# Two layers of a diffusion backbone: the first two copies of a batch of DRAM sums issued later, four modulation tiles taken from the gate-up run into the output run, and the first weight sum of retention issued amid the token sums

## The chip, the core and the metric

The kernel runs on one core of a Trainium2 chip. The metric is the time of one execution on the device in microseconds (us), lower is better. The engines are named as in the profile: PE multiplies matrices, DVE works on vectors, ACT casts and evaluates functions, POOL (here mostly an issuer of transfers) and SP (an issuer only) have instruction queues of their own, and 16 DMA engines move what all of them issue.

## The reference

Two layers over 512 latent tokens and 256 context tokens of width 1024, all in float32. Layer 0 mixes tokens by windowed attention, layer 1 by retention in four heads. Each layer has a SwiGLU feed-forward with 2816 hidden columns, and each is modulated by rows computed from the condition vectors.

```python
for i in range(DEPTH):
    mx = jnp.split(c_act @ ada_w[i] + ada_b[i], 6, axis=-1)     # latent stream
    mc = jnp.split(cc_act @ ada_w[i] + ada_b[i], 6, axis=-1)    # context stream
    h_x = modulate(rms_norm(x, norm1_g[i]), mx[0], mx[1])
    h_c = modulate(rms_norm(y_ctx, norm1_g[i]), mc[0], mc[1])
    out_c, out_x = windowed_gqa_sink(...) if i == 0 else bidir_retention(...)
    x = x + mx[2] * out_x
    x = x + mx[5] * swiglu(modulate(rms_norm(x, norm2_g[i]), mx[3], mx[4]), ffn_w_in[i], ffn_w_out[i])
    # the same for y_ctx with mc, in layer 0 only
return x
```

## The kernel before

**Arithmetic.** A float32 product is made of three matmuls: each operand is split into a high part (a cast, on ACT, line 171 of the profile: `whi` of a weight, `aq` or `sA` of tokens) and a low part (the operand less its high part, on DVE, line 172: `wlo` and so on), and high x high, low x high and high x low are added up. Large products are done by a seven-product scheme instead of eight, so sums of weight blocks and of token blocks are needed beside the blocks. Weight sums are formed in three ways: by DRAM to DRAM transfers ahead of their use (`gu_sum`, `fo_sum`: a copy at line 827, then accumulating transfers at line 830), by an accumulating load (`add_chunk`, issued on POOL), or by an addition on DVE.

**Stages.** The start loads x and the context, squares x on ACT, and reads the first modulation tiles (up to some 70 us). Attention follows, then the feed-forward of layer 0. Its gate-up half for hidden tiles 2 to 21 is the "seven run" (`seven(pos, jobs)`, line 1164, about 412 to 711 us): 20 positions of seven products of twelve matmuls each. After every second position the pair's sums are formed on DVE (`pair_sums`, line 1059, called from `last_gate` of the position after) and four transfers on POOL store them in DRAM (`saved`, lines 1069 and 1071). Its output half is the "output run" (the loop over `FO`, about 711 to 874 us): seven products of eleven hidden pairs, two pairs to a step, so that steps m = 0 to 4 have 24 matmuls and step m = 5 has 12. Step i+2 is split on ACT and DVE while step i runs on PE. Layer 1 follows: the retention heads (from about 874 us) and its feed-forward.

**The order.** In the seven run and the output run all engines run in the order in which the code is written (`manual_schedule`). In retention a scheduler sets the order, and `after(a, [b])` keeps a behind b.

**Sums in DRAM.** `spread(steps, turns)` lays the eight transfers of a batch of `fo_sum` out over turns. Turns from 100 on are positions of the seven run: the transfers of turn 100 + pos are issued on POOL at the end of position pos, behind whatever POOL was given before. The second batch (five pairs, 1280 KB a transfer) begins with two copies from the weights, which wait for nothing.

**Modulation tiles.** Layer 1 needs 48 tiles of 1024 x 128 of its modulation matrix (`ada_q`). The first 32 alternate between tiles for both streams (two DVE instructions at line 284) and for one stream (one). All go through a single buffer, `adaw`: `ada_next` reduces the tile that is there on DVE, and then issues the load of the next one, which waits until DVE has read the old one. The load is issued on SP in the seven run and on POOL in the output run. Position pos takes one tile in job 0 (after the third product) and one in job 2 (at its end); the output run takes one after the splits of each of the steps m = 0, 2 and 4 of its products 0 to 4.

**Retention, head 0.** `token_sums` forms the sums of token blocks on DVE, four rounds k = 0 to 3, each with a split into `sA`. Its Y product needs these and `w2`, the parts of r11 + q12, where r11 and q12 are weight chunks and q12 has been loaded and added to (`add_chunk`). In the profile the addition is line 1723, the further sums are lines 1726 and 1727, and the matmuls are line 1582. `strips` evaluates the decay rows (`dx`, `dcx`) on ACT, line 108, from a table `rj` that SP loads.

Of the kernel before, what the change touches and what calls it, by code (L numbers as in the profile page):

```python
# [54 lines left out]
def dit_kernel(ctx, tc, xT, cT, crow, small, consts, masks, tabs0, tabs1, jtab, adaQ, adaN, adaT, wst, wgu, wfo, out):  # L55
    nc = tc.nc
    mult, add, sub = ALU.mult, ALU.add, ALU.subtract
# [9 lines left out]
    def T(pool, cols, tag, bufs, dt=F32):  # L67
        return pool.tile([P, cols], dt, tag=tag, bufs=bufs, name=tag)
# [757 lines left out]
    def sum_copy(dst, src, behind):  # L826
        after((nc.gpsimd if by_hand[0] else nc.sync).dma_start(flat(dst), flat(src), max_dma_last_dim=ROW), [behind] if behind else [])

    def sum_add(dst, src, behind):
        after(nc.gpsimd.dma_start(flat(dst), flat(src), accum_op=add, max_dma_last_dim=ROW), [behind] if behind else [])  # L830
# [7 lines left out]
    def fo_steps(b):  # L838
        rows = slice(sum(FO_BATCHES[:b]), sum(FO_BATCHES[:b + 1]))
        t = fo_sum[b]  # L840
        return [lambda a: sum_copy(t[3], wfo[0, rows], a), lambda a: sum_copy(t[2], wfo[2, rows], a),
                lambda a: sum_add(t[3], wfo[2, rows], a), lambda a: sum_add(t[2], wfo[3, rows], a),
                lambda a: sum_copy(t[0], t[3], a), lambda a: sum_add(t[0], wfo[3, rows], a),
                lambda a: sum_copy(t[1], t[0], a), lambda a: sum_add(t[1], wfo[1, rows], a)]
# [3 lines left out]
    def spread(steps, turns):  # L848
        for st, n in zip(steps, turns):
            sum_turns.setdefault(n, []).append(st)  # L850
# [3 lines left out]
    spread(gu_steps(2), (4, 4, 6, 7))  # L854
    spread(gu_steps(3), (8, 8, 9, 10))
    spread(fo_steps(0), (11, 11, 13, 14, 16, 17, 19, 21))
    spread(fo_steps(1), (103, 103, 105, 107, 109, 111, 113, 115))

    for st in sum_turns[-1]:
        st(keys_end)  # L860
# [164 lines left out]
    def token_sums():  # L1025

        h1, h2 = THIRDS
        for k in range(4):
            t1, t2 = tm[k], tm[k + 4]
            for j in (k, k + 4):  # L1030
                nc.scalar.activation(tm[j][:, h1], tm[j][:, h1], AF.Identity, bias=mods[0, 0][:, 3, j:j + 1])
            nc.vector.tensor_tensor(t2[:, h2], t1[:, h2], t2[:, h2], op=sub)
            nc.vector.tensor_tensor(t1[:, h2], t1[:, h1], t1[:, h2], op=sub)
            nc.vector.tensor_tensor(t1[:, h1], t2[:, h2], t1[:, h1], op=sub)
            nc.vector.tensor_tensor(park[:, k * 384:(k + 1) * 384], t2[:, h1], t1[:, h1], op=add)
            for n, t in ((1, t2[:, h2]), (3, t1[:, h2]), (2, t1[:, h1])):
                S[n, k] = parts(quarter())
                split(t, *S[n, k])
# [80 lines left out]
    def ada_next(behind=()):  # L1119

        args = ada_q.pop(0)
        ada_tile(*args, cr, behind, fp, ada_w.pop())
        ada_ahead()
# [201 lines left out]
    ada_q = [t for pair in zip(ada_both, ada_one) for t in pair] + ada_one[16:]  # L1325
# [20 lines left out]
    h_rest, h_first, hm, early, ctx_sum = [], [], [], [], []  # L1346
# [86 lines left out]
    def chunk(i, own=False):  # L1433
        raw = T(qw, 1024, "wx", 4) if own else T(rp, 1024, "wraw", 2)
        nc.sync.dma_start(raw, wst[i])
        return raw

    def add_chunk(raw, i):
        nc.gpsimd.dma_start(raw, wst[i], accum_op=add)

    def split_chunk(raw, behind=()):
        w = w_parts(hpool[0])
        last_split[0] = split(raw, *w, behind)
        return w
# [8 lines left out]
    with tc.manual_schedule(engines=Hand):  # L1453
        by_hand[0] = True
        for pos in range(2, FT):
            jobs = [nothing] * 3
            if pos == 2:
                jobs = [last_sum, gates_negated, nothing]
            elif pos == 3:
                jobs[0] = rows_begin  # L1460
            elif pos == 4:
                jobs[2] = rows_silu
                ada_ahead()
            else:
                cr = row_t[0]
                jobs[0] = jobs[2] = ada_next
            if pos == FT - 1:
                def begin():
                    fo_split_weights(0)
                    fo_split_tokens(0)  # L1470
                    fo_split_tokens(1)
                jobs[1] = begin
            end = seven(pos, jobs)
            for st in sum_turns.get(100 + pos, ()):
                st(None)
        fo_y = [bank("Y"), bank("Z"), bank("Z"), bank("Y")]
        o = fo_y
        for i, (prod, m) in enumerate(FO):
            if m == 0 and prod:
                o = fo_y if prod in (2, 4) else fo_z if prod == 5 else [bank("X"), bank("X"), pj(384), pj(384)] \  # L1480
                    if prod in (1, 3) else [bank("Y"), bank("Z"), bank("Z"), bank("Y")]
                if prod == 3:
                    fo_z = o
            if i == 0:
                fo_split_weights(1)
                last_gate(FT - 1)
            if i + 2 < len(FO) and i + 4 != len(FO) and i + 3 != len(FO):
                fo_split(i + 2)
            last = i == len(FO) - 2
            fo_step(i, o, prod in (0, 1, 3, 6), last)  # L1490
            if m == (PAIRS - 1) // 2:
                for args in (((0, 0),), ((0, 0),), ((4, 0, True),), ((4, 1),), ((4, 1, True), (0, 1)), ((4, 0),), ())[prod]:
                    fo_add(o, *args)
            if prod < 5:
                ada_next() if m % 2 == 0 and ada_q else None
            elif prod == 5:
                early_sums(m)
            else:
                late_sums(m)
            if last:  # L1500
                break
            if i == 2:
                Q.close()
                H = ExitStack()
                hpool[0] = H.enter_context(tc.tile_pool(name="hR", bufs=1, reuse_waits="tile", side="right"))
                h_rest += [(T(hpool[0], 512, "aq", 11, F32R), T(hpool[0], 512, "aq", 11, F32R)) for _ in range(4)]
                h_first += [T(hpool[0], 512, "aq", 11, F32R) for _ in range(3)]
                off_grid(hpool[0], 16)
                h_first.insert(0, T(hpool[0], 512, "aq0", 1, F32R))
                hm += [T(hpool[0], 512, "qk", 8) for _ in range(KT)]  # L1510
        fo_add(o, 0, 1)
        last_square = last_squares()
        b11.append(split_chunk(b11.pop()))
        by_hand[0] = False
# [10 lines left out]
    qp = R.enter_context(tc.tile_pool(name="qp", bufs=1, reuse_waits="tile"))  # L1525
# [3 lines left out]
    h_sum = [(T(hS, 512, "sA", 16, F32R), T(hS, 512, "sA", 16, F32R)) for _ in range(KT)]  # L1529
# [8 lines left out]
            return lambda k: first(4 * (n[1] == "2") + k, int(n[0]) - 1)  # L1538
        return of

    def token_sums(hm, part, sh2, sums, behind=(), ops=(add, sub)):

        q1, q2 = HALVES
        shift = mods[1, 0][:, part]
        plus, minus = ops
        nc.vector.tensor_tensor(sh2[:, 0:4], shift[:, 0:4], shift[:, 4:8], op=plus)
        for k in range(4):
            t1, t2 = hm[k], hm[k + 4]
            after(nc.vector.scalar_tensor_tensor(t2[:, q2], t1[:, q2], sh2[:, k:k + 1], t2[:, q2], add, plus), behind)
            nc.vector.tensor_tensor(t1[:, q2], t1[:, q1], t1[:, q2], op=sub)  # L1550
            nc.vector.scalar_tensor_tensor(t1[:, q1], t2[:, q2], shift[:, k:k + 1], t1[:, q1], sub, sub)
            mid = split(t1, *sums[2 * k + 1])
            nc.vector.scalar_tensor_tensor(t2[:, q1], t2[:, q1], shift[:, k + 4:k + 5], t1[:, q1], add, minus)
            other_sums.append((t2, *sums[2 * k]))
        return mid

    def other_parts():
# [112 lines left out]
    normed, other_rms = ends  # L1670
    latent_norm(1, range(KT))
    for hd in range(RH):
        bq = chunk_base + 16 * hd
# [17 lines left out]
            other_values()  # L1691
        r11, r21 = chunk(bq), chunk(bq + 1)
        k11, k21 = split_chunk(r11), split_chunk(r21)
        if hd == 0:
            sums = token_sums(hm, 0, T(qp, 16, "sh2", 1), h_sum, [normed], (sub, add))
            dx, dcx = strips(0, [sums], [other_rms])
        cos1, sin1 = rope_tables()
        Y, X, kc = W4("Y"), W4("X"), W4("X")
        kt, qt = [[T(qa, 512, "gate", 4) for _ in range(2)] for _ in range(2)]
# [18 lines left out]
            context_keys()  # L1718


        q12, q22 = chunk(bq + 2, True), chunk(bq + 3, True)
        add_chunk(q12, bq + 3)
        nc.vector.tensor_tensor(r11, q12, r11, op=add)
        w2 = split_chunk(r11, () if hd else [sums])
        other_parts()
        nc.vector.tensor_tensor(r21, r21, r11, op=add)
        nc.vector.tensor_tensor(r11, r11, q22, op=sub)
# [26 lines left out]
        g12, w2, w4 = [], [], []  # L1754
# [125 lines left out]
        if not last:  # L1880
            dx, dcx = strips(hd + 1)
# [79 lines left out]
        hm = [T(hM, 512, "hm", 8) for _ in range(KT)]  # L1961
# [49 lines left out]
    sh2 = T(fp, 48, "sh2", 1)  # L2011
# [272 lines left out]
```

## Time and profile before

| quantity | value |
|---|---|
| median of three runs | 1715.09 us (1711.99 to 1717.15) |
| time of the profiled execution | 1720.03 us |
| span in its profile | 1718.3 us |
| mean granted PE clock | 0.993 |
| PE busy | 1681.1 us, 98% of the span |
| DVE busy | 1340.4 us, 78% |
| ACT busy | 891.7 us, 52% |

Busy time counts work and not waiting. A row of the timeline gives start, duration, engine, line and operation, what is written <- what is read, and in brackets how long the engine stood idle before it and what released it. Rows of the waits sum such idle time: total, times, longest. Rows of the transfers give the issuing queue, the count, the size of one, and the time from issue to landing. In rows by stretch each engine has its busy time, then come the granted PE clock, the busy share of the DMA engines and what they moved in GB/s.

### The profile page before, as it was taken

The page shows a single profiled execution, that of the slowest core. Times are in us where ns is not written, and L with a number is a line of the kernel's source. Part 1 is how long each engine was busy: PE and PEld are TensorE (multiplying, and loading weights), DVE is VectorE, ACT ScalarE, POOL GpSimd, SP SyncE. Part 2 cuts the span into 40 slices and gives each one's busy share as a digit, 9 for nine tenths or more (in the row PEclk, how much of TensorE's full clock was granted, in tenths as well). Part 3 has the DMA queues.
Part 4 walks back from the last instruction along what each step waited for, and adds up shares of the span by engine and source line. Part 5 has one row for each costly group of instructions (what it writes and reads, how often), then busy time and mean ns, then how long its engine had stood idle before and what let it go on. Part 6 is the DMA issues. An engine that isn't in the chain of part 4 may idle for free.

```text
span 1718.3 us, 27884 instructions
## 1 busy us (share of the span) xinstructions
PE 1681.1 (98%) x10798; PEld 1524.0 (89%) x10798; DVE 1340.4 (78%) x2395; ACT 891.7 (52%) x1565; POOL 101.2 (6%) x219
## 2 busy tenths in 40 slices
PE   6999999999999999999999999999999999999999
PEld 3888887889999999999988888898898999999997
DVE  4798888788687988877789757757767898877774
ACT  4587888656444434444665534534535565444442
POOL 0001111000110100100000000000000000000000
PEclk8999999999999999999999999999999999999999
DMA  9849885634787786898653725624724324333322
GB/s 365 310 137 198 214 186 155 218 118 167 210 264 224 249 233 206 290 309 287 216 163 76 207 76 125 178 69 123 196 62 111 111 74 123 99 119 103 98 87 86
DMA packets 112036, 293.87 MB, mean 171 GB/s; under 512 B 9520, under 2 KB 20288, under 8 KB 111648
## 3 DMA queue, kind: packets, MB, share of 16 engines
q1 hardware_dynamic: 89536, 229.77, 41.0%
q0 software_dynamic: 22080, 61.81, 15.9%
q8 instruction: 84, 1.38, 0.3%
q10 hardware_dynamic: 288, 0.52, 0.1%
q14 instruction: 48, 0.39, 0.1%
HBM read 274.82 MB, written 61.28 MB: 196 GB/s over the span
## 4 chain that ended last, share of the span: by engine, by line
PE 81%; DMA 8%; DVE 7%; ACT 3%; issue 2%; DVEq 0%; SPq 0%; ACTq 0%
PE Y L971 13%; PE Z L971 7%; PE Z L1593 6%; PE pj L154 5%; PE pj L156 5%; PE pj L155 5%; PE Y L1582 3%; PE X L971 3%; PE Y L1266 2%; PE Z L1266 2%; PE S L727 2%; PE pT L753 2%; PE pO L775 2%; DVE wlo L172 2%; PE pj L1266 2%; PE X L1266 2%
## 5 line engine op out<-in xcount | busy, mean ns | idle before, releaser
L171 ACT CAST whi<-wraw 128x1024 fp32r<-128x1024 f32 (+1 forms) x284 | 294.1, 1040 | 302.6 <-PE Y L971 70.6
L172 DVE TENSOR_TENSOR wlo<-wraw,whi 128x1024 fp32r<-128x1024 f32 (+1 forms) x284 | 342.3, 1209 | 113.2 <-ACT whi L171 112.2
L971 PE MATMUL Y<-aq,whi 128*128 128x384 f32 x640 | 172.8, 335 | 0.0
L971 PEld LDWEIGHTS Y<-aq,whi 128*128 128x128 f32 x640 | 116.6, 188 | 0.0
L971 PE MATMUL Y<-aq,wlo 128*128 128x384 f32 x320 | 107.6, 336 | 4.5 <-DVE wlo L172 4.5
L284 DVE CUSTOM_DVE_ANT_0 y<-adaw,crow,small_sb 128x1024 bf16<-128x1024 f32 x64 | 82.1, 1282 | 31.7 <-DMA adaw<-in_adaT_dram 31.1
L1593 PE MATMUL Z<-whi,sA 128*128 128x512 f32 x256 | 80.7, 391 | 0.0
L108 ACT ACTIVATE pr<-pr,stat,qs 128x513 f32<-128x513 f32 (+2 forms) x96 | 74.1, 774 | 11.2 <-DVE stat L734 11.1
L154 PE MATMUL pj<-ax,whi 128*128 128x512 f32 x176 | 69.2, 393 | 0.9 <-DVE res L263 0.6
L156 PE MATMUL pj<-ax,whi 128*128 128x512 f32 x176 | 68.7, 390 | 0.0
L155 PE MATMUL pj<-ax,wlo 128*128 128x512 f32 x176 | 68.6, 390 | 0.0
L971 PEld LDWEIGHTS Y<-aq,wlo 128*128 128x128 f32 x320 | 60.2, 188 | 5.8 <-DVE wlo L172 5.8
L263 DVE SCALAR_TENSOR_TENSOR res<-pj,mod,res 128x512 f32<-128x512 f32 (+1 forms) x64 | 45.3, 713 | 16.9 <-PE pj L156 16.9
L971 PE MATMUL Y<-sA,whi 128*128 128x256 f32 x304 | 58.4, 277 | 0.0
L753 PE MATMUL pT<-const_sb,pr 128*128 128x128 f32 x352 | 56.3, 285 | 2.1 <-DVE pr L744 1.0
L728 DVE CUSTOM_DVE_ANT_0 pr<-S,mask,qs 128x256 f32<-128x256 f32 (+1 forms) x96 | 53.4, 568 | 5.3 <-PE S L727 4.4
L1593 PEld LDWEIGHTS Z<-whi,sA 128*128 128x128 f32 x256 | 48.0, 188 | 10.4
L971 PE MATMUL Y<-hx,whi 128*128 128x256 f32 x304 | 56.5, 278 | 0.0
L1266 PE MATMUL Y<-aq,whi 128*128 128x384 f32 x176 | 52.9, 337 | 0.0
L1266 PE MATMUL Z<-aq,whi 128*128 128x384 f32 x176 | 51.4, 334 | 0.0
L1593 PE MATMUL Z<-wlo,sA 128*128 128x512 f32 x128 | 50.5, 394 | 0.5 <-DVE wlo L172 0.5
L753 PEld LDWEIGHTS pT<-const_sb,pr 128*128 128x128 f32 x352 | 41.2, 145 | 11.1 <-issue 4.3
(602 smaller groups left out, 5086.3 us busy)
## 6 DMA issues: line engine op xcount, KB each, us to landing
wraw<-in_wst_dram SPq DMA_DIRECT2D x157, 512.0 KB, 3.7
adaw<-in_adaT_dram SPq DMA_DIRECT2D x39, 512.0 KB, 3.8
op<-saved SPq DMA_DIRECT2D x35, 384.0 KB, 5.4
saved<-op POOLq DMA_DIRECT2D x33, 384.0 KB, 3.6
wraw<-in_wgu_dram SPq DMA_DIRECT2D x24, 512.0 KB, 4.5
gu_sum<-in_wgu_dram SPq DMA_DIRECT2D x8, 1280.0 KB, 13.0
gu_sum<-in_wgu_dram POOLq DMA_DIRECT2D x8, 1280.0 KB, 12.9
wraw<-fo_sum SPq DMA_DIRECT2D x20, 512.0 KB, 4.9
```

Source lines behind the costliest of these rows:

```text
L108: ins = nc.scalar.activation(*args, **kw)
L154: nc.tensor.matmul(o, whi, xhi, start=first, stop=False)
L155: nc.tensor.matmul(o, wlo, xhi, start=False, stop=False)
L156: return nc.tensor.matmul(o, whi, xlo, start=False, stop=last)
L171: after(nc.scalar.copy(hi, t), behind)
L172: return nc.vector.tensor_tensor(lo, t, hi, op=sub)
L284: res.append(nc.vector.tensor_tensor_reduce(junk, w, cr[:, s * 1024:(s + 1) * 1024], 1.0, sm_t[:, C_ADAB + l * 48 + j:C_ADAB + l * 48 + j ...
L728: nc.vector.tensor_tensor_reduce(pt[:, c0:c0 + w], bank, mask[:, m0:m0 + w], 1.0, top, add, ALU.min, lo)
L753: nc.tensor.transpose(tp[:, a * P:(a + 1) * P], self.pr[(0, 2, 1, 3)[a]][:, ki * P:(ki + 1) * P], ident)
L971: nc.tensor.matmul(o, p, r, start=first and k + i == 0, stop=k == 3 and i == 2, skip_group_check=not first)
L1266: nc.tensor.matmul(o[d], p[:, ws], r, start=first and k + e == 0, stop=k == PAIRS - 1 and e == 2, skip_group_check=True)
L1593: ins = nc.tensor.matmul(os[t], p, r, start=first and k + i == 0, stop=k == 3 and i == 2, skip_group_check=by_k or not first)
```

## The change

Three edits, independent of each other.

1. The second batch of `fo_sum` is one turn later in each of its eight transfers.
2. Positions 7, 9, 13 and 17 of the seven run no longer take a modulation tile in job 0. The output run takes one more, behind step m = 3, in products 0 to 3.
3. In head 0 the weight sum (loads of q12 and q22, addition to r11, split) is called out of `token_sums` after its round k = 1; before, it stood behind the first three products and its cast behind all of `token_sums`. The strips' later rows wait for `normed` instead of `other_rms`.

```diff
-    spread(fo_steps(1), (103, 103, 105, 107, 109, 111, 113, 115))
+    spread(fo_steps(1), (104, 104, 106, 108, 110, 112, 114, 116))
...
-                jobs[0] = jobs[2] = ada_next
+                jobs[2] = ada_next
+                if pos not in (7, 9, 13, 17):
+                    jobs[0] = ada_next
...
-                ada_next() if m % 2 == 0 and ada_q else None
+                ada_next() if ada_q and (m % 2 == 0 or m == 3 and prod < 4) else None
...
-    def token_sums(hm, part, sh2, sums, behind=(), ops=(add, sub)):
+    def token_sums(hm, part, sh2, sums, behind=(), ops=(add, sub), amid=None):
...
+            if amid and k == 1:
+                amid()
         return mid
...
+        qx, w2 = [], []
+
+        def weight_sum():
+            qx.extend((chunk(bq + 2, True), chunk(bq + 3, True)))
+            add_chunk(qx[0], bq + 3)
+            nc.vector.tensor_tensor(r11, qx[0], r11, op=add)
+            w2.extend(split_chunk(r11))
+
         if hd == 0:
-            sums = token_sums(hm, 0, T(qp, 16, "sh2", 1), h_sum, [normed], (sub, add))
-            dx, dcx = strips(0, [sums], [other_rms])
+            sums = token_sums(hm, 0, T(qp, 16, "sh2", 1), h_sum, [normed], (sub, add), weight_sum)
+            dx, dcx = strips(0, [sums], [normed])
...
-        q12, q22 = chunk(bq + 2, True), chunk(bq + 3, True)
-        add_chunk(q12, bq + 3)
-        nc.vector.tensor_tensor(r11, q12, r11, op=add)
-        w2 = split_chunk(r11, () if hd else [sums])
+        if hd:
+            weight_sum()
+        q12, q22 = qx
```

**POOL's queue.** The difference on POOL, first at the program's start and then in the seven run; `off` are small constants, `saved` the stores of a pair, `fo_sum_1179` the second batch.

```order
 L237 MEMSET off_541 128x48
 L237 MEMSET off_544 128x16
-L827 DMA fo_sum_1179<-in_wfo_dram 640x512 x2
 L237 MEMSET off_978 128x16
 L711 COPY pr<-qs 128x1 x10
...
 L1069 DMA saved_4632<-op 128x2x384 x4
 L1071 DMA saved_4632<-op 128x384
-L830 DMA fo_sum_1179<-in_wfo_dram 640x512
+L827 DMA fo_sum_1179<-in_wfo_dram 640x512 x2
 L1069 DMA saved_4633<-op 128x2x384 x3
 L1071 DMA saved_4633<-op 128x384
```

Before, the two copies stand at the very start of the program: they wait for nothing, and no instruction that is ordered by hand stands ahead of them on POOL. Now they stand behind the second pair's stores, where the first accumulating transfer stood, and each later transfer stands one pair further on.

**DVE's queue in the output run.** Product 0 of the output run before, from its step m = 2 on: `wlo` and `aq` are the low parts of a step's weights and tokens, the two rows at line 284 one modulation tile, line 1285 the additions of the product to the residual.

```order
1183 L284 ISA y_8130,mod_76<-adaw,crow,small_sb 128x1024
1184 L284 ISA mod_76 128x1
1185 L172 TENSOR_TENSOR wlo<-wraw,whi 128x512
1186 L172 TENSOR_TENSOR aq<-op,aq 128x384
1187 L172 TENSOR_TENSOR wlo<-wraw,whi 128x1024
1188 L172 TENSOR_TENSOR aq<-op,aq 128x768
1189 L284 ISA y_8232,mod_76<-adaw,crow,small_sb 128x1024
1190 L284 ISA mod_76 128x1
1191 L172 TENSOR_TENSOR wlo<-wraw,whi 128x1024
1192 L172 TENSOR_TENSOR aq<-op,aq 128x768
```

The same place now:

```order
1175 L284 ISA y_8114,mod_76<-adaw,crow,small_sb 128x1024
1176 L284 ISA mod_76 128x1
1177 L172 TENSOR_TENSOR wlo<-wraw,whi 128x512
1178 L172 TENSOR_TENSOR aq<-op,aq 128x384
1179 L284 ISA y_8180,mod_76<-adaw,crow,small_sb 128x1024
1180 L284 ISA mod_76 128x1
1181 L172 TENSOR_TENSOR wlo<-wraw,whi 128x1024
1182 L172 TENSOR_TENSOR aq<-op,aq 128x768
1183 L284 ISA y_8220,mod_76<-adaw,crow,small_sb 128x1024
1184 L284 ISA mod_76 128x1
1185 L172 TENSOR_TENSOR wlo<-wraw,whi 128x1024
1186 L172 TENSOR_TENSOR aq<-op,aq 128x768
```

A third tile stands between the split of the half step (128x512) and the split of the next product's first step. The tile of step 0 of product 0, ahead of these rows, is now one for both streams where it was one for one stream.

**DVE's queue in head 0.** The token sums before (lines 1549 to 1553, splits into `sA` at line 172) and the weight sum behind them:

```order
1384 L172 TENSOR_TENSOR sA<-qk,sA 128x512
1385 L1553 SCALAR_TENSOR_TENSOR qk<-qk,mod_76 128x256
1386 L172 TENSOR_TENSOR sA<-qk,sA 128x512
1387 L1621 TENSOR_TENSOR hn<-hn,rj 128x256
1388 L1723 TENSOR_TENSOR wraw<-wx,wraw 128x1024
1389 L1622 TENSOR_TENSOR dx<-hn 128x128
1390 L172 TENSOR_TENSOR sA<-qk,sA 128x512
1391 L1726 TENSOR_TENSOR wraw<-wraw 128x1024
1392 L172 TENSOR_TENSOR wlo<-wraw,whi 128x1024
```

The place in the token sums where the same addition (now line 1703) and its split stand now:

```order
1376 L1555 SCALAR_TENSOR_TENSOR qk<-qk,mod_76 128x256 x2
1377 L172 TENSOR_TENSOR sA<-qk,sA 128x512
1378 L1703 TENSOR_TENSOR wraw<-wx,wraw 128x1024
1379 L172 TENSOR_TENSOR sA<-qk,sA 128x512
1380 L1551 SCALAR_TENSOR_TENSOR qk<-qk,sh_9921 128x256 x2
1381 L1552 TENSOR_TENSOR qk<-qk 128x256
1382 L172 TENSOR_TENSOR wlo<-wraw,whi 128x1024
1383 L1553 SCALAR_TENSOR_TENSOR qk<-qk,mod_76 128x256
```

The addition and the low part of its result (line 172, `wlo`) stand amid rounds 2 and 3 of the token sums, ahead of the strips' products (line 1621 before).

## The prediction

> **What bounds the kernel now.** I read the page's engine rows and chain first, then the waits of PE stage by stage, then, where PE waits, what ended that wait.
>
> ```profile
> PE 1681.1 (98%) x10798; PEld 1524.0 (89%) x10798; DVE 1340.4 (78%) x2395; ACT 891.7 (52%) x1565; POOL 101.2 (6%) x219
> PE 81%; DMA 8%; DVE 7%; ACT 3%; issue 2%; DVEq 0%; SPq 0%; ACTq 0%
> ```
>
> PE is busy 98% of the span, 37 us idle in all. The change touches no matmul, so it can gain or lose only where PE stands still or would stand still. Three places matter. The first is the start: the transfers of the first 70 us, two windows, and what PE waited for up to 120 us.
>
> ```profile
> DMA packets 8947, 26.20 MB, mean 374 GB/s; under 512 B 942, under 2 KB 1326, under 8 KB 8940
> q0 software_dynamic: 672, 2.62, 10.4%
> fo_sum<-in_wfo_dram POOLq DMA_DIRECT2D x2, 1280.0 KB, 13.9
> 15.00:20.00 5.00, 0.00 (x0) 0.00 (x0) 0.69 (x1) 1.02 (x2) 0.00 (x0) 0.55 1.01 383
> 30.00:50.00 20.00, 19.23 (x269) 15.73 (x269) 15.04 (x38) 9.89 (x21) 0.00 (x0) 1.00 1.02 395
> PE pT L227 <- DVE y L220: 9.7, 1, 9.7
> ```
>
> All DMA engines are busy, and PE waits 9.7 us for the sum of squares; ACT's last square shows why:
>
> ```profile
> 19.61 0.63 ACT L219 ACTIVATE hs<-res 128x512 f32<-128x512 f32 x1 [2.75 <-DMA res<-in_xT_dram]
> 21.02 2.08 PE L227 MATMUL pT<-y,ones_sb 128*128 128x512 f32 x2 [9.66 <-DVE y L220]
> 23.02 3.27 PE L356 MATMUL pT<-adan,ccol 128*32 128x128 f32 x64
> ```
>
> It waits for x itself. From 23 us on PE is nearly dense (19.23 of 20 us), so its start sets when it gets through.
>
> The second place is the output run. PE never waits in its middle, but DVE does, for modulation tiles; the window of one product, DVE's waits from 700 to 850 us, and the tile loads from 711 to 826 us:
>
> ```profile
> 734.00:757.00 23.00, 23.00 (x134) 23.00 (x134) 18.93 (x25) 10.10 (x13) 1.85 (x4) 1.00 0.91 308
> DVE y L284 <- DMA adaw<-in_adaT_dram: 9.5, 6, 3.0
> adaw<-in_adaT_dram POOLq DMA_DIRECT2D x14, 512.0 KB, 4.5
> ```
>
> The third is head 0, in PE's waits from 840 to 1010 us and three windows behind the longest, with the clock down to half:
>
> ```profile
> PE Y L1582 <- DVE wlo L172: 1.6, 1, 1.6
> PE Y L1582 <- ACT gate L1736: 0.8, 1, 0.8
> PE Y L1582 <- ACT whi L171: 0.6, 1, 0.6
> 912.00:914.00 2.00, 1.73 (x12) 1.73 (x13) 2.00 (x4) 0.06 (x2) 0.00 (x0) 0.81 0.00 0
> 914.00:916.00 2.00, 2.00 (x11) 2.00 (x11) 2.00 (x3) 1.04 (x1) 0.00 (x0) 0.50 0.00 0
> 916.00:918.00 2.00, 2.00 (x17) 2.00 (x17) 0.96 (x3) 1.22 (x2) 0.00 (x0) 0.84 0.39 59
> ```
>
> **Part 1, the copies leave the start.** They are all of POOL's 2.62 MB in the first 70 us and land 13.9 us after issue, while x is still being loaded. At 0.374 to 0.42 MB per us (the mean rate, and the best of the early windows) the bytes are 6.2 to 7.0 us of the engines' time; their share, 10.4% of 70 us, is 7.3. I take 6.5 off the time at which x, and every load behind it, lands: −6.5 us, from −5 (ACT's squares have work of their own between the waits) to −8.5.
>
> The low end of that range has this behind it: the granted clock is 0.55 from 15 to 20 us, where PE idles, and the first matmuls after it run slowly. A wait of 3 us in place of 9.7 may keep the clock up; L227 and L356 are 5.3 us together, so at most some 2 us come on top. The Trainium skill, TensorE: Matmul & The Clock Gate, Part 1, has the clock fall to half after an idle window of about 3.4 us; the trace agrees, with 0.55 behind 9.66 us of idling, and by that rule a wait of 3 us could go either way.
>
> The copies now run at about 449 us, where one accumulating transfer ran:
>
> ```profile
> 448.70 1.20 POOL L830 DMA_DIRECT2D fo_sum<-in_wfo_dram  x1
> L284 DVE CUSTOM_DVE_ANT_0 y<-adaw,crow,small_sb x64: 1277/1284/1286, 461.8 to 814.6; 128x1024 bf16<-128x1024 f32 x64
> 489.02 1.28 DVE L284 CUSTOM_DVE_ANT_0 y<-adaw,crow,small_sb 128x1024 bf16<-128x1024 f32 x1 [4.02 <-DMA adaw<-in_adaT_dram]
> PE Y L971 <- DVE wlo L172: 4.5, 4, 1.8
> ```
>
> Two copies move twice one transfer's bytes. The first tiles are read from 462 us, so a backlog until then costs at most a delay of 0.5 us; I take +0.5, from 0 to 1. The further transfers each move one pair on. Where they meet a pair's stores, a tile lands late, DVE waits (4.02 us at 489), the split behind it is late and PE waits: 4.5 us in four places in the whole run (the last row, 400 to 720 us). Position 16 gets such a meeting for the first time; by the others it is +1.
>
> **Part 2 in the seven run.** The dropped job-0 tiles come right behind the waiting tile of the position before, so they take none of those four waits away. They change which tiles are single: in positions 8, 14, 15 and 16 the first is now single and the second double. The second's load starts 1.28 us earlier and its reduction takes 1.28 longer, which cancels. Dropping four loads lightens the DMA engines a little: −1. The seven run's sum with position 16: 0, from −2.5 to +3.
>
> **Part 2 in the output run.** A tile's cycle, from rows of DVE and POOL:
>
> ```profile
> 718.34 1.28 DVE L284 CUSTOM_DVE_ANT_0 y<-adaw,crow,small_sb 128x1024 bf16<-128x1024 f32 x1
> 719.93 0.56 POOL L275 DMA_DIRECT2D adaw<-in_adaT_dram  x1 [1.93 <-DVE mod L284]
> 726.63 1.28 DVE L284 CUSTOM_DVE_ANT_0 y<-adaw,crow,small_sb 128x1024 bf16<-128x1024 f32 x1 [2.99 <-DMA adaw<-in_adaT_dram]
> 728.76 0.54 POOL L275 DMA_DIRECT2D adaw<-in_adaT_dram  x1 [8.28 <-DVE wlo L172]
> 734.47 1.28 DVE L284 CUSTOM_DVE_ANT_0 y<-adaw,crow,small_sb 128x1024 bf16<-128x1024 f32 x1 [2.99 <-DMA adaw<-in_adaT_dram]
> 735.67 1.22 DVE L172 TENSOR_TENSOR wlo<-wraw,whi 128x1024 fp32r<-128x1024 f32 x1
> 736.81 0.95 DVE L172 TENSOR_TENSOR aq<-op,aq 128x768 fp32r<-128x768 f32 x1
> 743.37 0.53 POOL L275 DMA_DIRECT2D adaw<-in_adaT_dram  x1 [6.78 <-DVE mod L284]
> 747.50 1.28 DVE L284 CUSTOM_DVE_ANT_0 y<-adaw,crow,small_sb 128x1024 bf16<-128x1024 f32 x1 [0.41 <-DMA adaw<-in_adaT_dram]
> ```
>
> With one buffer, the next load is issued 1.6 us after a tile's start (718.34 to 719.93), and the next tile can start 0.1 us after its landing. At the median landing of 4.5 us a cycle is 6.2 us. A product on PE is 132 matmuls of 23.00/134 = 0.172 us, about 22.8 us (4.15 a step, half that for the half step). Three cycles, 18.6 us, fit; four, 24.8, do not. The quoted waits of DVE show the scatter from issue to next tile: 719.93 to 726.63 is 6.7 us, 728.76 to 734.47 5.7, 743.37 to 747.50 4.1.
>
> The output run starts here:
>
> ```profile
> 711.20 0.33 PE L1266 MATMUL Y<-aq,whi 128*128 128x384 f32 x1
> ```
>
> The shortage reaches PE, since DVE takes its queue in order: the split of the next product's step 0 stands behind the new tile, and that of its step 1 behind the fourth. Worked once, for product 0 and landings of 4.5: tile m2 starts at 719.93 + 4.5 + 0.1 = 724.5, its successor's load is issued 2.1 later (as at 726.63 to 728.76), so the new tile starts at 731.3 and the split behind it ends at 731.3 + 1.2 + 1.15 + 0.9 = 734.6, where PE wants it at 711.2 + 22.8 = 734.0. The fourth tile starts 6.2 later, at 737.5; the split of step 1 ends at 740.7, where PE, 0.6 late by then, wants it at 738.8. Some 2 us more of waiting, and the next product begins as late.
>
> I replayed the five products so, step by step (DVE in order; 1.14 us for the low part of weights by the starts of the rows at 735.67 and 736.81, 0.87 for that of tokens, whose 0.95 overlaps the next; half for the half step; PE starting a step when both are there). With the landings of the trace the replay gives tiles at 726.6, 734.5, 747.5 and 755.1, the rows' own times, and no wait of PE, as in the profile. With four tiles PE's waits come to:
>
> ```
> landing, us      3.8   4.0   4.25  4.5   4.75  5.0
> PE waits, us     3.5   5.9   8.9  11.9  15.4  18.8
> ```
>
> With the trace's scatter of landings in place of one value it is 14 to 23, 18 in the middle, since a late tile costs and an early one gives little back. I take +12: the run is stretched by about a tenth, so the engines, at 0.91 here, are a little freer for each load. Clock dips behind such waits fall into the next wait and add nothing. The double tile in product 0 adds 1.28 us of DVE: +1. Together +13, from +4 to +20.
>
> **Part 3, head 0.** Rows of DVE and ACT before:
>
> ```profile
> 907.92 1.22 DVE L1723 TENSOR_TENSOR wraw<-wx,wraw 128x1024 f32<-128x1024 f32 x1
> 910.99 1.23 DVE L172 TENSOR_TENSOR wlo<-wraw,whi 128x1024 fp32r<-128x1024 f32 x1
> 915.07 1.22 DVE L172 TENSOR_TENSOR wlo<-wraw,whi 128x1024 fp32r<-128x1024 f32 x1
> 886.52 0.71 ACT L108 ACTIVATE dx<-rj,dcol 128x384 f32<-128x384 f32 x1 [2.31 <-DMA rj<-in_jtab_dram]
> ```
>
> The addition at 907.92, its cast and its low part are what PE waited for twice (0.6 and 1.6). They now come during X's product, and these waits go. The next weights' low part, at 915.07 + 1.22 = 916.3, moves up by about 2.5 us (1.22 + 1.23), as the addition and the low part ahead of it are done; so the copy of Y that held PE for 0.8 comes earlier too. The dip of the clock behind the waits (0.81, 0.50 and 0.84 in three windows of 2 us: 2 x (0.19 + 0.50 + 0.16) = 1.7 us) goes with them. ACT's 2.31 us of waiting for the table of the decay rows, with the casts behind it, also goes, since those rows now come later. The waits and the dip are 0.6 + 1.6 + 0.8 + 1.7 = 4.7; of this I let 0.9 come back, since DVE has the same work to do in the same stretch: −3.8, from −4.7 to −1.5.
>
> **The sum.** −6.5 + 0.5 + 0 + 13 − 3.8 = +3.2 us. The profiled execution, 1720.0, would become 1723.2; it is 4.9 above the median of the runs, and I set the same difference on the median: 1715.1 + 3.2, about 1718. What a measurement of this kernel can tell from no change is about 0.3%, 5.1 us.
>
> **The rivals.** The sum without the landings' term is 1 − 9.8 = −8.8 us, so the mean landing decides: 3.7 us or less gives faster by over 5.1, 4.65 or more slower by over 5.1.
>
> *Slower, by landings as they scatter.* One mechanism: in the output run, tile loads share the engines with step loads, as the 5.7 to 6.7 us above, and each late tile holds the splits behind it. +18 in place of +12 gives +9, 1724; it decides from a mean landing of 4.65 us. For: two of the three quoted gaps from issue to tile are far above the median. Against: a stretched run asks less of the engines per us.
>
> *Faster, by short landings.* With four loads spread over a longer product, landings of 3.8 to 4.0 give 3.5 to 5.9, and a clock kept up at the start another −2: −5 to −7, about 1709. For: one gap quoted above is 4.1 us, and loads of the same tile on SP land so, in the whole program:
>
> ```profile
> adaw<-in_adaT_dram SPq DMA_DIRECT2D x39, 512.0 KB, 3.8
> ```
>
> Against: 0.91 of the engines' time is taken in the output run.
>
> *The copies hold nothing up.* If x's loads kept their pace whatever POOL moves, part 1 would be worth 0 and the whole +9.7, 1725. Against it: full engines, and 13.9 us for 1.28 MB. The Trainium skill, DMA: Bandwidth & Descriptors, Queues, rings and completion order, says that an engine takes turns between its queues packet by packet; the trace agrees, with both queues moving side by side in those 14 us, and by that rule the copies take their share from x.
>
> **How the numbers follow.** The forecast, within 0.3%, takes landings of 3.8 to 4.6 and part 1 as costed: 0.37. Slower by over 0.3% is 0.35: 0.29 for scattered landings, 0.06 for copies that held nothing up. Faster is 0.28, by short landings and by sizes at the good ends of parts 1 and 3. The range goes from 1706, the faster rival with part 1 at −8.5, to 1727, the slower one with position 16 at +3.
>
> **What would show it.** Right: PE's first sum of squares (L227) at about 14.5 us; tiles in the output run 6 us apart and DVE waiting for them 30 us or more in all; PE waiting for `wlo` in steps 0 and 1 of products 1 to 4, about 3 us a product; Y's product in head 0 without the waits of 0.6 and 1.6. Wrong: PE dense through the output run, or L227 still near 21 us.

## The result, and the profile after

The changed kernel takes 1721.24 us (median of 6 runs, 1716.83 to 1723.45) against 1713.47 us of the kernel before in the same runs (6 runs, 1710.18 to 1717.15): 7.8 us more, a ratio of 1.004 with a 95% interval of 1.0021 to 1.0059. The time lies within the range given, 3 us above the forecast. It is a small loss, at the edge of what the 0.3% of the prediction can tell from no change.

Its profiled execution took 1723.45 us, the longest of the six. The page's first row, then the rows of PE's matmuls in the seven run and the output run (count, shortest/median/longest in ns, first and last start in us):

```profile
PE 1684.6 (98%) x10798; PEld 1523.2 (88%) x10798; DVE 1341.1 (78%) x2395; ACT 891.7 (52%) x1565; POOL 104.5 (6%) x223
L971 PE MATMUL Y<-aq,whi x640: 334/334/525, 402.0 to 705.2; 128*128 128x384 f32 x160
L1266 PE MATMUL Y<-aq,whi x176: 334/334/526, 705.4 to 882.6; 128*128 128x384 f32 x176
```

The busy shares say almost nothing: PE is busy 98% of the span before and after. The first and last starts of a stage say much, and I cut every profile at the same four places: the first matmul of the seven run, the first and the last of the output run, and the first of the last feed-forward (L154). Stages in us, with the kernels of the experiments, which are told below:

| kernel | start | seven run | output run | retention | rest |
|---|---|---|---|---|---|
| before | 412.6 | 298.6 | 163.1 | 534.2 | 309.8 |
| before, a second profile | 409.8 | 294.6 | 163.0 | 533.7 | 309.1 |
| changed | 402.0 | 303.4 | 177.2 | 530.2 | 308.6 |
| changed, a second profile | 401.4 | 300.9 | 176.9 | 530.5 | 308.6 |
| first edit alone (e1) | 402.5 | 299.0 | 163.1 | 533.9 | 310.6 |
| second edit alone (e2) | 408.8 | 299.6 | 176.3 | 533.9 | 308.6 |
| third edit alone (e3) | 409.4 | 296.7 | 163.0 | 531.0 | 309.6 |
| first and third (e4) | 402.6 | 296.8 | 163.0 | 530.2 | 310.4 |
| changed, four tiles not loaded (e5) | 401.6 | 303.6 | 163.1 | 530.0 | 309.9 |
| changed, four loads not waited for (e6) | 401.2 | 299.8 | 163.1 | 530.7 | 308.9 |
| before, copies behind x (e7) | 410.7 | 293.3 | 163.1 | 534.5 | 310.1 |
| first and third, sums held (e8) | 402.1 | 299.1 | 163.1 | 529.8 | 308.6 |
| changed, kinds of tiles put back (e9) | 401.7 | 298.8 | 178.5 | 531.0 | 308.6 |
| first and third, tile behind the splits (e10) | 401.1 | 301.0 | 165.3 | 530.3 | 310.7 |

Start, output run and retention repeat to a microsecond or so from profile to profile where the code is the same (the start with the copies in it to 4 us). The seven run scatters by 4 us with the same code, so one profile of it says little.

**The start.** The transfers of the first 70 us, the window from 10 to 15 us, and PE:

```profile
DMA packets 8649, 24.93 MB, mean 356 GB/s; under 512 B 960, under 2 KB 1344, under 8 KB 8640
10.00:15.00 5.00, 5.00 (x64) 2.79 (x66) 2.08 (x3) 3.36 (x6) 0.00 (x0) 1.00 1.03 419
12.53 1.04 PE L227 MATMUL pT<-y,ones_sb 128*128 128x512 f32 x2
13.49 1.97 PE L356 MATMUL pT<-adan,ccol 128*32 128x128 f32 x64
```

PE comes to the sum of squares at 12.5 instead of 21.0 us, without a wait, and the clock is 1.00 there: L227 and L356 take 3.0 us instead of 5.3.

**The seven run.** PE's wait, two of the six places that make it up, and the windows behind these two:

```profile
PE Y L971 <- DVE wlo L172: 8.6, 6, 2.8
603.77 0.44 PE L971 MATMUL Y<-aq,wlo 128*128 128x384 f32 x1 [2.75 <-DVE wlo L172]
636.79 0.45 PE L971 MATMUL Y<-aq,wlo 128*128 128x384 f32 x1 [2.03 <-DVE wlo L172]
604.00:608.00 4.00, 4.00 (x17) 4.00 (x17) 3.08 (x5) 1.56 (x3) 0.00 (x0) 0.66 0.88 303
636.00:640.00 4.00, 3.21 (x18) 3.21 (x19) 2.81 (x4) 0.99 (x3) 0.00 (x0) 1.00 0.89 250
```

Before it was 4.5 us in four places. All six places are alike: PE stands in the third product of an odd position, before a split that stands on DVE behind the last tile of the even position ahead. I name each by the position of that tile. The wait at 603.77 is position 14; the one at 636.79 is position 16, where a sum now meets a pair's stores.

**The output run.** PE's and DVE's waits, the tile loads, and the run as one window:

```profile
PE X L1266 <- DVE wlo L172: 3.7, 2, 3.2
PE Y L1266 <- DVE aq L172: 1.4, 4, 0.4
PE Y L1266 <- DVE wlo L172: 1.4, 3, 0.6
PE X L1266 <- DVE aq L172: 1.0, 3, 0.4
DVE y L284 <- DMA adaw<-in_adaT_dram: 33.6, 14, 4.7
adaw<-in_adaT_dram POOLq DMA_DIRECT2D x18, 512.0 KB, 4.2
705.40:882.60 177.20, 169.09 (x934) 164.09 (x933) 134.54 (x204) 82.38 (x117) 12.47 (x23) 0.98 0.77 260
```

DVE waits 33.6 us for tiles where it was 9.5, and PE waits 7.5 us for the splits behind them where the profile before has no such wait. At the end of product 0, on DVE and then on PE:

```profile
722.54 1.29 DVE L284 CUSTOM_DVE_ANT_0 y<-adaw,crow,small_sb 128x1024 bf16<-128x1024 f32 x1 [3.39 <-DMA adaw<-in_adaT_dram]
...
729.56 1.28 DVE L284 CUSTOM_DVE_ANT_0 y<-adaw,crow,small_sb 128x1024 bf16<-128x1024 f32 x1 [4.65 <-DMA adaw<-in_adaT_dram]
730.77 0.08 DVE L284 DVE_READ_ACCUMULATOR2_ANT mod<- 128x1 f32 x1
730.77 1.22 DVE L172 TENSOR_TENSOR wlo<-wraw,whi 128x1024 fp32r<-128x1024 f32 x1
731.91 0.95 DVE L172 TENSOR_TENSOR aq<-op,aq 128x768 fp32r<-128x768 f32 x1
735.12 1.29 DVE L284 CUSTOM_DVE_ANT_0 y<-adaw,crow,small_sb 128x1024 bf16<-128x1024 f32 x1 [2.25 <-DMA adaw<-in_adaT_dram]
```

```profile
732.05 0.69 PE L1266 MATMUL X<-aq,wlo 128*128 128x384 f32 x1 [3.22 <-DVE wlo L172]
```

Read together: the second tile starts at 722.5, the new one 7.0 us later at 729.6, and directly behind it stand the low parts of product 1's first step, which PE has been waiting for since 728.8. Behind that wait the clock falls:

```profile
732.00:736.00 4.00, 3.77 (x11) 3.37 (x12) 1.75 (x2) 0.07 (x1) 0.00 (x0) 0.50 0.90 285
736.00:740.00 4.00, 4.00 (x18) 4.00 (x17) 4.00 (x8) 0.45 (x1) 0.53 (x1) 0.70 0.63 219
```

**Head 0.** PE's wait in Y's product, the window with it, and the addition on DVE:

```profile
PE Y L1586 <- DVE wlo L172: 0.9, 1, 0.9
920.00:922.00 2.00, 1.12 (x9) 0.84 (x7) 2.00 (x4) 2.00 (x4) 0.00 (x0) 1.00 0.00 0
908.88 1.22 DVE L1703 TENSOR_TENSOR wraw<-wx,wraw 128x1024 f32<-128x1024 f32 x1
```

Of the three waits, 3.0 us, 0.9 is left, and the clock stays at 1.00.

### The profile page after: what moved, and what is told of

Read it like the earlier page. It is cut to its first block, busy times and chain, and to the rows that moved or that the text cites. A ratio compares the mean times of both kernels' runs of the same rounds, so it can differ in the third digit from the quotient of the medians.

```text
span 1721.4 us, 27879 instructions
## 1 busy us (share of the span) xinstructions
PE 1684.6 (98%) x10798; PEld 1523.2 (88%) x10798; DVE 1341.1 (78%) x2395; ACT 891.7 (52%) x1565; POOL 104.5 (6%) x223
## 4 chain that ended last, share of the span: by engine, by line
PE 44%; DVE 6%; DMA 3%; issue 1%; ACT 1%; POOL 0%; DVEq 0%; ACTq 0%; SPq 0%; POOLq 0%
PE Y L971 6%; PE Z L1597 6%; PE Z L971 3%; PE Y L1586 3%; PE pj L154 2%; PE pj L156 2%; PE pj L155 2%; DMA adaw<-in_adaT_dram 2%; PE pj L1597 2%; PE X L971 2%; PE X L1586 1%; DVE wlo L172 1%; DMA wraw<-in_wst_dram 1%; PE X L1597 1%; PE Z L1266 1%
## 5 line engine op out<-in xcount | busy, mean ns | idle before, releaser
L154 PE MATMUL pj<-ax,whi 128*128 128x512 f32 x176 | 69.2, 393 | 0.5 <-DVE res L263 0.3
## 6 DMA issues: line engine op xcount, KB each, us to landing
gu_sum<-in_wgu_dram SPq DMA_DIRECT2D x8, 1280.0 KB, 12.6
```

The lines of the kernel that those rows point to most:

```text
L154: nc.tensor.matmul(o, whi, xhi, start=first, stop=False)
```

## The experiments

**Each edit alone, and the first with the third.** The diffs are the parts of the change shown above.

> Only the first edit: the second batch of sums one turn later. Theory: x and all loads behind it land earlier, so the start is 6.5 (the bytes) to 10.6 us (as the two profiles show it, with a cold clock in the one before) shorter; the transfers that meet other pairs' stores in the seven run cost 2 to 3 us more waiting of PE. Time 1705 to 1710, PE's first product with the sum of squares at about 12.5 us. Rival: the copies held nothing up in ordinary executions, and the start gain is one of the profiled execution alone: 1713 to 1716.

1706.27 us (6 runs) against 1714.5: ratio 0.9958 (0.9943 to 0.9973). L227 starts at 13.21 us. The gain is there in ordinary executions.

> Only the second edit: four modulation tiles taken out of the seven run into the output run. Theory: four tile cycles of about 6 us don't fit into a product of 22.8 us, so the output run grows by 12 to 15 us, and the seven run stays within 1 us: 1725 to 1729. Rival: the growth of the output run needs the later sums of the first edit too, or the seven run gains from its four dropped loads what the output run loses: below 1720.

1734.54 us (4 runs): ratio 1.0113 (1.0097 to 1.0129), 20 us more, above what the theory gave. The output run alone shows where; its window is

```profile
708.40:884.70 176.30, 168.42 (x934) 163.12 (x933) 133.73 (x204) 82.36 (x117) 12.50 (x24) 0.99 0.77 261
```

176.3 us without the first edit, so the late sums have no part in it. This profiled execution, 1729.2 us, was the fastest of its four runs, 5 us below their median; where those 5 us lie no profile shows.

> Only the third edit: the weight sum of head 0 amid the token sums. Theory: PE's waits in head 0 for the sum's high and low part and for the copy of Y go, with the clock dip behind them: 3.5 to 4.5 us less, 1709 to 1710, and PE's waits from the first of them on total 1 us or so. Rival: the waits only move to a later weight of the same head: 1712 to 1714.

1711.13 us (11 runs): ratio 0.9977 (0.9968 to 0.9986), 3.4 us less, just under the 3.5 to 4.5 of the theory. Retention takes 531.0 us instead of 534.

> The changed kernel with the second edit undone: late copies and the early weight sum. Theory: the parts add up, so this is the sum of the first and the third run's differences, 1701 to 1706, and 15 to 18 us below the changed kernel. Rival: part of the loss in the seven run comes from the later sums and remains: 1707 to 1712.

1702.89 us (5 runs): ratio 0.9937 (0.9924 to 0.9949), 11.6 us less, which is 8.2 + 3.4 of the first and third run. The parts add up: −8.2 + 20.0 − 3.4 = +8.4, and the whole change measured +7.8. This is the fastest kernel of the study, with e8 level with it, 18 us below the changed one.

**Why the output run grows.** The first kernel takes the extra tile from rows that are on the chip already:

```diff
-                ada_next() if ada_q and (m % 2 == 0 or m == 3 and prod < 4) else None
+                if m == 3 and prod < 4:
+                    ada_tile(*ada_q.pop(1), cr, (), fp, cr[:, 0:1024])
+                elif m % 2 == 0 and ada_q:
+                    ada_next()
```

> The changed kernel, but the four extra tiles of the output run are not loaded: DVE does the same reduction on rows that are there already (so four columns of the modulation are wrong), and three loads a product remain. Theory (tile cycle): DVE has nothing to wait for there, the output run is back at 163 to 165 us, and the whole at 1703 to 1708. Rival (DVE's own work of 1.28 us a tile between the splits): the output run stays above 172 us, the whole above 1714. The seven run keeps the edit of the tiles, so if its 303 us of the changed kernel are an effect of both edits and no accident, they are seen again.

The second adds a transfer behind that tile:

```diff
                 if m == 3 and prod < 4:
                     ada_tile(*ada_q.pop(1), cr, (), fp, cr[:, 0:1024])
+                    nc.gpsimd.dma_start(flat(gu_sum[prod][0, 0:2]), flat(wgu[2, 0:2]), max_dma_last_dim=ROW)
```

> As the kernel without the four loads, but with a transfer of the same 512 KB in place of each, into a buffer in DRAM that nobody reads later, issued on the same queue. Theory (tile cycle): what costs is that DVE waits, not the traffic, so the output run is 163 to 167 us and the whole within 3 us of the kernel without loads. Rival (traffic): the loads of steps and of the other tiles land later, the output run is at 170 us or more.

The first: 1708.22 us (10 runs), 7.1 below the kernel before beside it (1715.29), ratio 0.9966 (0.9953 to 0.998). The second: 1704.94 us (4 runs), ratio 0.9938 (0.9921 to 0.9954). The output runs as windows, without the loads:

```profile
705.20:868.30 163.10, 162.72 (x935) 161.78 (x934) 134.60 (x204) 82.40 (x117) 10.30 (x19) 1.00 0.79 270
DVE y L284 <- DMA adaw<-in_adaT_dram: 4.5, 6, 1.3
```

and with loads that nobody waits for, with those four transfers:

```profile
701.00:864.10 163.10, 162.72 (x935) 161.78 (x934) 134.23 (x204) 82.40 (x117) 12.53 (x23) 1.00 0.82 283
gu_sum<-in_wgu_dram POOLq DMA_DIRECT2D x4, 512.0 KB, 7.2
```

DVE has as much work as in the changed kernel (134.6 and 134.2 us against 134.5), the engines move more in the second (283 GB/s against 260), and the output run is back at 163.1, to the tenth. The totals miss the theory's bands by 0.2 and 0.3 us; the output runs lie within theirs. Neither DVE's work nor the traffic costs anything in the output run. What costs is that DVE stands in its queue before a tile that has not landed. With the loads taken away, the changed kernel's difference to the kernel before goes from +7.8 to −7.1: 14.9 us.

**Whether x alone holds the start.** In the kernel before, the two copies go to SP's queue behind x:

```diff
     nc.sync.dma_start(cst, consts)
+    for n, r in ((3, 0), (2, 2)):
+        nc.sync.dma_start(flat(fo_sum[1][n]), flat(wfo[r, FO_BATCHES[0]:sum(FO_BATCHES)]), max_dma_last_dim=ROW)
...
-    spread(fo_steps(1), (103, 103, 105, 107, 109, 111, 113, 115))
+    spread(fo_steps(1)[2:], (105, 107, 109, 111, 113, 115))
```

> The kernel before, but the two copies are issued on SP's queue behind the loads of x, so that x lands first and all later loads come behind the copies. Theory (every load counts): PE's sum of squares starts at 12 to 13 us, but the matmuls that read the last modulation tiles (L326) start no earlier than about 58 us, since their loads are as late as before: 1712 to 1715. Rival (only x counts): they start at about 51 us, and the time is that of the late copies, 1705 to 1708.

1714.27 us (10 runs) against 1715.29: ratio 0.9995 (0.9986 to 1.0004), no difference. PE's waits up to 75 us, and two rows of PE (L356 of the kernel before is L362 here):

```profile
PE pT L362 <- DMA adan<-in_adaQ_dram: 7.2, 3, 6.8
12.57 1.13 PE L227 MATMUL pT<-y,ones_sb 128*128 128x512 f32 x2 [0.70 <-DVE y L220]
20.48 1.80 PE L362 MATMUL pT<-adan,ccol 128*32 128x128 f32 x24 [6.78 <-DMA adan<-in_adaQ_dram]
```

PE starts as early as in the changed kernel and then stands 6.8 us before the next load. Its matmuls with the last tiles start at 60.8 us, where the other four profiles with the copies at the start have 58.2 to 61.2 and those with late copies 50.8 to 51.6. Every load of the start counts, whichever it is that the copies delay.

**What the seven run's growth is.** The first of three kernels holds each later transfer of the sums, in the kernel of e4, to the end of its position:

```diff
+            if pos > 4 and 100 + pos in sum_turns:
+                nc.gpsimd.tensor_copy(spare[:, 0:1], tile[pos]["a"][0][:, 0:1])
             for st in sum_turns.get(100 + pos, ()):
                 st(None)
```

> The kernel with the first and third edit alone, in which the accumulating transfers of the second batch also wait, by a small POOL copy of the position's result, for the end of the position, so that they run in the position without stores. Theory (meeting of a pair's stores, the sum and a tile load): PE's waits of 3.6 us in the seven run fall to 1.5 or less, and the time to 1698 to 1701. Rival (the stores alone, or the sums wherever they run, make the tiles late): 1702 to 1705, with as many waits in odd positions.

1703.96 us (6 runs), ratio 0.9933 (0.992 to 0.9945), level with e4. The rival's wait is as large as ever, now in odd positions:

```profile
PE Y L972 <- DVE wlo L173: 4.5, 4, 2.1
```

So it isn't the meeting with the stores alone: moved into the positions without stores, the sums of 1280 KB make tiles late there. The second kernel is the changed one with the queue of tiles reordered, so that second tiles of even positions are single again:

```diff
-    ada_q = [t for pair in zip(ada_both, ada_one) for t in pair] + ada_one[16:]
+    ada_q, both, one = [], list(ada_both), list(ada_one)
+    for pos in range(5, FT):
+        drop = pos in (7, 9, 13, 17)
+        ada_q += [] if drop else [both.pop(0)]
+        ada_q.append(both.pop(0) if drop and pos < 17 else one.pop(0))
+    ada_q += one
```

> The changed kernel, but the queue of tiles is reordered so that the second tile of every even position is single again, as before the edit, and double tiles stand only in first jobs and in odd positions. Theory: the growth of the seven run (303 us in the changed kernel and in the one without loads, against 297 to 299 with the tiles in place) comes from the double second tiles, which hold the split behind them 1.28 us longer while the load lands no earlier; the seven run is 297 to 299 us, PE's wait near 604 us falls from 2.75 to about 1, and the time is 4 to 6 us below the changed kernel, 1715 to 1718. Rival: the kinds cancel as forecast and the growth is scatter of the transfers: 301 to 304 us, 1719 to 1723.

1720.13 us (10 runs), ratio 1.0024 (1.0012 to 1.0036): 5.2 us above the kernel before beside it, where the changed kernel was 7.8 above its own, and the intervals of the two overlap. The seven run is 298.8 us, as the theory had it, but the wait that should have shrunk is there:

```profile
602.13 0.45 PE L971 MATMUL Y<-aq,wlo 128*128 128x384 f32 x1 [2.57 <-DVE wlo L172]
```

The theory of the double tiles isn't borne out for this wait, which is position 14's; the one of position 16 is 0.3 us here. The third kernel, again that of e4, reads the second tile of an even position behind the next position's first two splits:

```diff
         split(t["u"], *b3)
+        late_job.pop()() if late_job else None
...
-                jobs[0] = jobs[2] = ada_next
+                jobs[0] = ada_next
+                if pos % 2 or pos == FT - 1:
+                    jobs[2] = ada_next
...
             end = seven(pos, jobs)
+            if pos > 4 and pos % 2 == 0:
+                late_job.append(ada_next)
```

> The kernel with the first and third edit alone, in which the second tile of each even position is read on DVE behind the next position's first two splits and not ahead of them. Theory: PE's waits in the seven run come only from these splits standing behind a tile whose load is late, so all of them (3.6 us, and the clock dips behind them) go: seven run 292 to 294 us, time 1697 to 1700. Rival: the tile in the next position's first job, now some 4 us behind, waits for its load and hands the delay on to the later splits: no better than 1703.

1708.17 us (10 runs), ratio 0.9967 (0.9955 to 0.9978), 5 us worse than e4; the seven run has 301.0 us where e4 has 296.8, the output run 165.3 instead of 163.0. DVE's wait for tiles in the seven run and PE's for splits:

```profile
DVE y L284 <- DMA adaw<-in_adaT_dram: 32.2, 8, 5.8
```

```profile
PE Y L971 <- DVE wlo L172: 6.3, 7, 1.3
```

The rival was right: the next tile, 4 us behind, waits up to 5.8 us for its load, and holds the splits behind it instead. It is the tile cycle of the output run, at another place.

**How far one profile can be trusted.** Both kernels once more:

> The kernel before once more, for its profile. If the start of the profile shown (seven run begins at 412.6 us) was a slow instance, it begins near 409 us here, as in the two other kernels that keep the copies at the start (408.8 and 409.4), and the gain of the late copies is 6.5 to 7.5 us as costed from the bytes; if not, at 412 to 413. The seven run: 297 to 300 us if it scatters little, else outside.

> The changed kernel once more, for its profile. If the 303.4 us of its seven run belong to the kernel, 302 to 305 us again, with waits of PE of 2 us or more near 604 and 637 us; if they are scatter of the transfers, 298 to 301 us. The output run: 176 to 180 us either way.

The kernel before took 1712.01 us; its start is 409.8 us, so the 412.6 of the first profile lies at the top of what the copies at the start give, and its seven run 294.6, below the band. The changed kernel took 1720.17 us, with 300.9 in the seven run, which is in the band of scatter, and 176.9 in the output run. PE's waits in its seven run stand at the same six positions as in the first profile, though the two longest are shorter:

```profile
PE Y L971 <- DVE wlo L172: 7.8, 6, 2.0
```

## Why the prediction was right or wrong

**Start: right in mechanism, sized too small.** Forecast −6.5. The four profiles with the copies at the program's start (before twice, e2, e3) reach the seven run at 410.2 us in the mean, the nine with late copies at 401.8: −8.4, at the edge of the range given. In the same profiles L227 starts at 19.5 and at 12.6 us in the mean, 6.9 us earlier, near the 6.5 of the bytes. L227 and the first run of L356 then take 5.0 and 3.3 us in the mean, 1.7 us less. This goes with the clock, which the prediction held back as "at most some 2 us": it was 0.55 from 15 to 20 us in the profile before and is 1.00 from 10 to 15 us in the changed one. No run separates the clock from the bytes. The prediction let a wait of 3 us remain in place of 9.7; at most 1.0 us remains in the nine. One reading was too narrow: "It waits for x itself", and that PE's "start sets when it gets through". With x early and the copies behind it (e7), PE waits 6.8 us for the next load and reaches the seven run at 410.7. The rival that the copies hold nothing up is out by e1.

**Cost of the copies at 449 us: right.** They are issued at 438.2 us in the changed kernel, whose start is shorter, and PE's first wait in the seven run ends at 480.3, 42 us later.

**Seven run: wrong.** Forecast 0, from −2.5 to +3. The seven runs of the change (changed twice, e5, e6) have a mean of 301.9 us, those of the code before (before twice, e3) 296.6: +5.3, and a little more if e7's 293.3 is counted in. PE's waits there are 8.0 us in the mean of the four profiles and 3.4 in that of the three, so 4.6 of the 5.3 us are waiting. Two of the waits make up most of it, and each goes with one edit. The wait of position 14 goes with the second: it is 1.9 to 3.7 us in the six profiles with the tiles moved (changed twice, e2, e5, e6, e9) and 0.5 to 1.0 us in six with the tiles in place (before twice, e1, e3, e4, e7; e8 and e10 shift the waits to odd positions). The second edit alone and the first with the third:

```profile
609.28 0.69 PE L971 MATMUL Y<-aq,wlo 128*128 128x384 f32 x1 [2.63 <-DVE wlo L172]
599.94 0.44 PE L971 MATMUL Y<-aq,wlo 128*128 128x384 f32 x1 [0.58 <-DVE wlo L172]
```

The wait of position 16 goes with the first: 1.3 to 2.0 us in six profiles with the later sums (changed twice, e1, e4, e5, e6), 0.3 in e9, and none with the sums where they were (before twice, e2, e3, e7).

So the step that failed is the one that lets the moved tiles cost the seven run nothing: "which cancels", and the −1 for four loads less. In position 14 of the changed kernel the load is issued 1.3 us behind the start of the first tile, and 2.6 us in the kernel before, so it does start earlier, as forecast. But its tile is read 8.7 to 10.4 us after the issue in the six profiles with the tiles moved, against 7.7 to 8.2 in the six others. The kinds of the tiles aren't the reason, since e9 puts them back and keeps the wait (2.57 us); why this load is slower stays open. Position 16, forecast at +1, was right in place and is 1.6 us in the mean. The other waits change from profile to profile, and how they share the rest isn't settled.

**Output run: right in mechanism; the size fits, but not by the replay alone.** Forecast +13, measured 14.1, 13.9 and 13.2 us in the profiles of the table, and 15.4 in that of e9 (178.5 us). The tile cycle is what e5 and e6 show, and the replay's place of the waits is the trace's: the first steps of the products. The growth lies in products 1 to 4. The median landing was 4.2 us, for which the replay alone gives 8, and single loads were later, such as the one of 5.4 us from 724.1 to 729.5; what these add wasn't computed. By the window PE is idle for 8.1 of the 177.2 us, and for 0.4 in the run without the loads. So the waits that the profile shows are about as long as the replay's, and they do not make up the 14.1 alone. The sign named beforehand, about 3 us of waiting a product, came out at 7.5 us in four products. One assumption isn't settled: that dips of the clock behind the waits "add nothing". Worked out from windows of 2 us, what PE's clock falls short of 1.00 in the output run comes to 3.4 us in the changed kernel, 1.7 in its second profile and in e2, and 0 in e9, whose output run is the longest of the four all the same. The slower rival's 18 us was too much in the profiles; in the median of e2, 5 us above its profile, it isn't excluded.

**Head 0: right.** Forecast −3.8; retention is 3.2 to 4.0 us shorter in the two profiles of each kernel, and the edit alone gives 3.4 us on the medians. What comes back was put at 0.9, and 0.9 us of waiting is left.

**The sum.** Forecast +3.2; the stages give −8.4 + 5.3 + 13.7 − 3.6 = +7.0, the medians +7.8. The table's last stage is 0.9 us shorter in the changed profiles, which has no term and no cause shown; with it the stages give +6.1. The two terms that were off, the start by −1.9 and with +0.5 not seen, and the seven run by +5.3, have opposite signs. That the total is nearer than its parts is luck. The likeliest case, within 0.3%, was narrowly missed by the median (0.45%), and the interval reaches across the bound.

## What to carry to other kernels

A buffer that is loaded only after it has been read has a cycle, issue plus landing plus use, and a stage of fixed length holds so many cycles and no more. One more delays whatever is queued behind it on the engine that waits: here a fourth cycle of about 6 us in a product of 22.8 us cost 13 to 15 us over four products, and the same work and the same traffic without the wait cost nothing. Transfers that nobody needs for hundreds of microseconds cost 8.4 us in a start whose DMA engines are full, and issuing them on another queue, behind the first loads, left that cost as it was. A change of three edits is best measured edit by edit: here two that gain 11.6 us together were hidden by a third that costs 18 to 20.

## What the runs showed that was not expected

PE's clock fell behind shorter waits than expected, and not behind every one. In the windows behind the waits of the changed kernel, after the wait of 3.22 us at 732 it was 0.50, after 2.75 us at 604 0.66, but after 2.03 us at 637 1.00; before the change a wait of 1.80 us at 522.7 was followed by

```profile
524.00:526.00 2.00, 2.00 (x9) 2.00 (x8) 1.43 (x3) 0.55 (x2) 0.00 (x0) 0.53 0.94 291
```

The Trainium skill, TensorE: Matmul & The Clock Gate, Part 1, gives an idle window of about 3.4 us, free-running; here 1.80 us of idling was enough once, and 2.03 us was not another time, so the length of a wait alone doesn't tell whether the clock falls.
